# A two-layer Mamba-2 and attention trunk: engines issue in the source's order, with the source laid out anew

## The chip, the cores and the metric

The kernel runs on one core of a Trainium2 chip. The metric is the device time of one execution in microseconds (us). The engines are PE (TensorE, the matrix multiplier, with its weight loads as PEld), DVE (VectorE), ACT (ScalarE), POOL (GpSimd) and SP (SyncE, which here only issues transfers). Every engine works through its own list of instructions in order. A list is fixed when the kernel is built; at run time an instruction waits for semaphores that others raise.

## The reference, cut to what matters

256 tokens of width 2048 pass a Mamba-2 layer and an attention layer, all in float32.

```python
# layer 0: Mamba-2 mixer, then x <- LayerNorm(ALPHA * x + mixer(x))
zxbcdt = x @ w_in                                   # z | x, B, C | dt
xbc = silu(causal_conv4(xbc) + conv_b)
dt = softplus(dt_raw + dt_bias); a = -exp(a_log)
y = ssd_chunked(xs, dt, a, bm, cm) + xs * d_skip    # decays from a cumulative sum of dt * a
y = y * silu(z)
y = y * rsqrt(mean(y**2 within a group) + EPS) * norm_w   # 8 groups
h = y @ w_out
# layer 1: one shared k, v; window of 128 with a sink per head
k, v = x @ kv_w + kv_b;  k = rope(k)
q, gate = x @ w_in;      q = rope(q + q_bias)
h = (softmax_with_sink(q k / 8) v * silu(gate)) @ w_out
# and again x <- LayerNorm(ALPHA * x + h)
```

## The kernel before

**Products.** Every large product is made of three matmuls (`mac`, `out_unit`, `x_stat`): each float32 operand is split into a high part and a low remainder, and high x high, low x high and high x low are added in PSUM. The weights come as *units* of 128 x 2048. `load_unit` (line 122) loads a unit in two halves of 512 KB into `wr` (five buffers, issued by SP, L129), ACT writes the high part `wh` (L137), DVE the remainder `wl` (L138); there are four buffers of each. `next_unit` gives out the next unit, and `fill_units` before it keeps `AHEAD` = 2 units loaded and split beyond those given out.

**Layer 0** runs over eight groups. A group has ten input blocks of 128 columns, each one unit of 48 matmuls of 256 columns (`gemm_ws`): B, C, four x blocks, four z blocks (in group 0 the z blocks first). `conv_silu` evicts a B, C or x block: ACT once (L402), three shifted multiply-adds on DVE (L404), a tanh on ACT (L407), a last DVE operation (L408). `in_z` evicts a z block. A table `plan` names what comes after which block: step t = 10 g + b is block b of group g. In a group: the decays (`sum_decay`, `exp_decay` on ACT, from rows that a transfer has spread over the partitions, `load_decay`, `load_low`); `cb` (two small matmuls on PE, then `cbm` and two large `e` products on DVE, L483 and L486); the turned x times dt (group 0: `tr`, PE transposes L499; others: `turn_blocks`, `load_turned`, `scale_x` by DVE transposes and DRAM); `ymm` (PE, L550, evicted by DVE); `gate` (POOL products L566 to L572, then the split into `yH` on ACT and `yL` on DVE for each block in turn); `norm` (an inverse root by three Newton steps, twelve POOL operations L600 to L603 on 128 x 2). The out products of a group (four units of 24 matmuls of 512 columns, `out_unit`) run among the next group's blocks at `OUT_AT`; their eviction L302 needs the inverse root. PSUM has four `mm` buffers, taken in turn, and four `ax` buffers.

Group 0 begins in `products_first`: three units and the dt columns arrive in nine pieces; PE takes a piece's dt matmuls and then its products. `make_dt` follows: a softplus, a scan over time (L368), two transfers to DRAM (`rscr`), from which `load_decay` reads. `turn_dt` (step 6) transposes dt.

**The boundary.** After group 7 come three more out units of group 6, the norm of group 7, and its four out units in `out_last`: units in turn for row half 0 and, for the first, row half 1; `done1(0)`; the remaining units for half 1; `done1(1)`. `done1(h)` normalises the row half by pieces of 512 (L759, L762), transposes each on PE (L767) and splits it into `x1H` (ACT, L772) and `x1L` (DVE, L773). Then k and v: four units, half 0 and then half 1, 12 matmuls each (`x_stat`, L809 to L811).

**Layer 1** runs over `B_ORDER`: q blocks and gate blocks, out units, and the attention of each pair (`attend`), whose steps are put off by a number of ticks (`later`).

**What sets the order.** Before, each engine's list is laid out by a planner, which orders instructions by priority and its estimate of times; `tc.high_priority` (L401, L472, L644) moves some ahead, and `keep_in_program_order` holds a few. A buffer's next use waits for the release of its last one.

Of the kernel before, what the change touches and what calls it, by code (L numbers as in the profile page):

```python
# [15 lines left out]
P = 128  # L16
S = 256
# [8 lines left out]
AHEAD = 2  # L26

TD, TS, CB0 = 6, 6, 9
# [3 lines left out]
NZERO = 3  # L32
XK_AT = (12, 13)
ZPRI = 200
PRE = 1
CPRI = 0
# [24 lines left out]
def trunk(ctx: ExitStack, tc: tile.TileContext, A: dict, out: bass.AP, dbg=None):  # L61
# [53 lines left out]
    def new_unit(places):  # L115
        u = Unit()
        u.parts = []
        for tag, n, pl in (("wh", NH, places[0]), ("wl", NL, places[1])):
            t = wp.tile([P, 2112], F32R, tag=tag, name=nm(tag), bufs=n)
            u.parts.append([(t[:, o : o + (k1 - k0) * P], k0, k1) for o, k0, k1 in pl])  # L120
        u.h, u.l = u.parts[0][0][0], u.parts[1][0][0]
        return u

    def load_unit(src, places):
        u = new_unit(places)
        raws = []
        for c in range(2):
            raw = wp.tile([P, 1024], F32, tag="wr", name=nm("wr"), bufs=NR)
            nc.sync.dma_start(raw[:], src[:, c * 1024 : (c + 1) * 1024])  # L129
            raws.append(raw)  # L130
        for c in range(2):
            for (h, k0, k1), (l, _, _) in zip(*u.parts):
                a, b = max(k0, 8 * c), min(k1, 8 * c + 8)
                if a < b:
                    sl = slice((a - k0) * P, (b - k0) * P)
                    raw = raws[c][:, (a - 8 * c) * P : (b - 8 * c) * P]
                    nc.scalar.activation(h[:, sl], raw, AF.Copy)  # L137
                    nc.vector.tensor_tensor(l[:, sl], raw, h[:, sl].bitcast(F32), ALU.subtract)  # L138
        return u
# [25 lines left out]
    def products_first():  # L165
# [9 lines left out]
        nc.sync.dma_start(pc[:], A["pc"])  # L175
        fill_units()
        pss = [mm_tile() for _ in us]
        pd = ax_tile()
        for (k0, k1), raw in zip(FIRST, raws):
            for k in range(k0, k1):  # L180
                rows = slice(64 * (k % 2), 64 * (k % 2) + 64)
                nc.tensor.matmul(
                    pd[rows, :S], raw[:, k - k0, FCOL - NHD :], raw[:, k - k0, :S], start=k < 2, stop=k >= KT - 2
                )
# [7 lines left out]
        return pd, pss  # L192
# [13 lines left out]
    srcs += wo_srcs("wo", NG - 1) + [A["wkv"][i] for i in range(4)]  # L206
    broken = set()
    for what, j in B_ORDER:
        if what == "g":
            broken.update(range(len(srcs), len(srcs) + 4))  # L210
        srcs += wo_srcs({"q": "wq", "g": "wg", "o": "wb"}[what], j)
    units = []
    used = [0]

    def fill_units():
        while len(units) < min(used[0] + AHEAD, len(srcs)):
            n = len(units)
            if n == 4:
                nc.sync.dma_start(cc[:], A["cc"])
# [6 lines left out]
            units.append(load_unit(srcs[n], BROKEN if n in broken else [WHOLE, WHOLE]))  # L226

    def next_unit():
        used[0] += 1
        fill_units()  # L230
        return units[used[0] - 1]
# [104 lines left out]
    def make_dt(ps):  # L336
        f = [ap.tile([P, S], F32, tag="sm", name=nm("f"), bufs=NSM) for _ in range(3)]
        f4 = ap.tile([P, 4, S], F32, tag="xs", name=nm("f4"), bufs=1)
        u, e, rec, z = [f4[:, i, :] for i in range(4)]
        w, q, dt = [x[:] for x in f]  # L340
        nc.scalar.copy(e, ps[:, :S])
        both = ax_tile()
        nc.tensor.matmul(both[:, :S], fold, e, start=True, stop=True)
        nc.scalar.activation(u, both[:, :S], AF.Identity, bias=pc[:, PC_DTB : PC_DTB + 1])
        nc.scalar.activation(e, u, AF.Abs)
        nc.scalar.activation(e, e, AF.Exp, scale=-1.0)
        aneg = ap.tile([P, 1], F32, tag="aneg", name="aneg")
        nc.scalar.activation(aneg[:], pc[:, PC_ALOG : PC_ALOG + 1], AF.Exp)
        nc.vector.tensor_scalar(aneg[:], aneg[:], -1.0, None, ALU.mult)
        nc.vector.tensor_scalar(rec, e, 2.0, None, ALU.add)  # L350
        nc.vector.reciprocal(rec, rec)
        nc.vector.tensor_tensor(z, e, rec, ALU.mult)
        nc.vector.tensor_tensor(w, z, z, ALU.mult)
        nc.vector.tensor_scalar(q, w, 1.0 / 15.0, None, ALU.mult)
        nc.vector.tensor_scalar(z, z, 2.0, None, ALU.mult)
        for d in (13.0, 11.0, 9.0, 7.0, 5.0, 3.0):
            nc.vector.scalar_tensor_tensor(q, q, 1.0 / d, w, ALU.add, ALU.mult)
        nc.vector.scalar_tensor_tensor(q, q, 1.0, z, ALU.add, ALU.mult)
        nc.vector.scalar_tensor_tensor(dt, u, 0.0, q, ALU.max, ALU.add)
        da, hi = e, rec  # L360
        nc.vector.tensor_scalar(da, dt, aneg[:], None, ALU.mult)
        nc.vector.tensor_scalar(hi, da, QUANT, None, ALU.add)
        nc.vector.tensor_scalar(hi, hi, QUANT, None, ALU.subtract)
        nc.vector.tensor_tensor(hi[64:128], da[64:128], hi[64:128], ALU.subtract)
        one = z
        nc.gpsimd.memset(one, 1.0)
        rc = w
        nc.vector.tensor_tensor_scan(rc, one, hi, 0.0, ALU.mult, ALU.add)  # L368
        nc.sync.dma_start(rscr[0:64, :], rc[:64])

        nc.scalar.activation(hi[64:128], rc[64:128], AF.Exp)
        nc.sync.dma_start(rscr[64:128, :], hi[64:128])
        return rc, dt, q
# [21 lines left out]
    def conv_silu(ps, t, dst):  # L395
# [5 lines left out]
        with tc.high_priority(CPRI):  # L401
            nc.scalar.activation(a[:], ps[:, :S], AF.Identity, scale=w(3), bias=w(4))  # L402
            for sft in (1, 2, 3):
                nc.vector.scalar_tensor_tensor(  # L404
                    a[:, sft:], ps[:, : S - sft], w(3 - sft), a[:, sft:], ALU.mult, ALU.add
                )
        nc.scalar.activation(dst, a[:], AF.Tanh)  # L407
        nc.vector.scalar_tensor_tensor(dst, dst, 1.0, a[:], ALU.add, ALU.mult)  # L408
# [61 lines left out]
    def in_z(g, i, ps):  # L470
        z = ap.tile([P, S], F32, tag="zz", name=nm("z"), bufs=4)
        with tc.high_priority(ZPRI):  # L472
            nc.scalar.activation(z[:], ps[:, :S], AF.Tanh, scale=0.5)
            nc.vector.scalar_tensor_tensor(z[:], z[:], 1.0, ps[:, :S], ALU.add, ALU.mult)
# [34 lines left out]
    def turn_blocks(g):  # L509

        st = gs[g]
# [51 lines left out]
    def gate(g, i):  # L563
        st = gs[g]
        v = st.yz[:, i, :]
        nc.gpsimd.tensor_tensor(v, v, st.z[i][:], ALU.mult)  # L566
        q = ap.tile([P, S], F32, tag="sm", name=nm("sq"), bufs=NSM)
        nc.gpsimd.tensor_tensor(q[:], v, v, ALU.mult)
        if i == 0:
            st.ss = q  # L570
        else:
            nc.gpsimd.tensor_tensor(st.ss[:], st.ss[:], q[:], ALU.add)  # L572
        if i == 0:
            st.y = (
                yp.tile([P, 4, S], F32R, tag="yH", name=nm("yH"), bufs=2),
                yp.tile([P, 4, S], F32R, tag="yL", name=nm("yL"), bufs=2),
            )
        yH, yL = st.y
        c = PC_NW + g * 4 + i
        nc.scalar.activation(yH[:, i, :], v, AF.Copy, scale=pc[:, c : c + 1])  # L580
        nc.vector.scalar_tensor_tensor(
            yL[:, i, :], v, pc[:, c : c + 1], yH[:, i, :].bitcast(F32), ALU.mult, ALU.subtract
        )

    def norm(g):
# [13 lines left out]
        for _ in range(3):  # L599
            nc.gpsimd.tensor_tensor(t, r, r, ALU.mult)  # L600
            nc.gpsimd.tensor_tensor(t, t, v, ALU.mult)
            nc.gpsimd.tensor_scalar(t, t, -0.5, 1.5, ALU.mult, ALU.add)
            nc.gpsimd.tensor_tensor(r, r, t, ALU.mult)  # L603
        st.rms = r

    def group(g):
# [16 lines left out]
        if g == NG - 1:  # L623
            out_units(g - 1, [1])
            out_units(g - 1, [2, 3])
# [12 lines left out]
    dt_ps, first_ps = products_first()  # L638

    for c0, c1 in ((PC_CONV, PC_CONV + 240), (PC_NW, PC_NW + 32)):  # L640
        nc.vector.tensor_scalar(pc[:, c0:c1], pc[:, c0:c1], 0.5, None, ALU.mult)

    with tc.high_priority():
        dts = make_dt(dt_ps)  # L644
        load_decay(0, 0)

# [3 lines left out]

    def rotary():
        posi = ap.tile([P, 2], I32, tag="posi", name="posi")
        tc.keep_in_program_order(nc.gpsimd.dma_start(posi[:], A["pos"]))
        inv = ap.tile([P, 8], F32, tag="inv", name="inv")
        tc.keep_in_program_order(nc.gpsimd.dma_start(inv[:], A["inv"]))
# [33 lines left out]
    at(35, rotary)  # L689
    for g in range(NG):  # L690
        t = 10 * g
        if g == 0:
            at(TD, turn_dt, *dts)
            at(TS, load_decay, 0, 1)
            at(TS, load_low, 0)
            steps = TS
            pos = dict(cb=CB0, tr=12, y=13, norm=16)
# [24 lines left out]
        for i in range(4):  # L722
            at(t + pos["y"], gate, g, i)
# [22 lines left out]

    with ExitStack() as s2:
# [6 lines left out]
        def done1(h):  # L754
            mv, rs = norm_scale(lp, st1, h)
# [404 lines left out]
```

## Time and profile before

| what | value |
|---|---|
| median of 3 runs | 1000.1 us (999.4 to 1002.09) |
| the profiled execution | 1000.52 us |
| its span, first to last instruction | 998.7 us |
| mean granted TensorE clock | 0.995 |
| PE, DVE, ACT, POOL busy | 984.9, 776.9, 533.7, 202.6 us |

The span is the part of the execution that the profile shows; 1.8 us lie around it. A matmul's busy time includes its way through the array, and the next one starts before it has ended, so PE is counted as busy while it issues at full pace and also where its start-to-start interval is longer than it need be. A row of the table of windows reads: from and to, length, then busy us and count of PE, PEld, DVE, ACT and POOL, the granted clock, the share of the DMA engines and GB/s. A timeline row reads: start, us, engine, line, operation, tiles out<-in, shapes, count of merged instructions, and in brackets the idle time before it with what ended that.

### The profile page before, as it was taken

To read this page: it belongs to the slowest core of one execution; us is meant where nothing else is said; L and a number is where in the kernel's file an instruction comes from. 1 tells how busy PE (TensorE), PEld (TensorE's weight loads), DVE (VectorE), ACT (ScalarE), POOL (GpSimd) and SP (SyncE) were. 2 spreads that over 40 slices of the span, in tenths; PEclk is the share of its full clock that TensorE was granted. 3 is DMA by queue.
4 is the path that set the end of the run, shared out by engine and by line. 5 is a ranking of instruction groups with operands and counts; after the bars stand their busy time and mean duration, and the time that the engine had idled before them with its cause. 6 is when DMAs were issued, how large, how long until landed. Compare 5 with 4: busy or idle time off the path is not lost.

```text
span 998.7 us, 17607 instructions
## 1 busy us (share of the span) xinstructions
PE 984.9 (99%) x6836; PEld 880.7 (88%) x6836; DVE 776.9 (78%) x1147; ACT 533.7 (53%) x901; POOL 202.6 (20%) x321
## 2 busy tenths in 40 slices
PE   9999989999999999999999999999999999999997
PEld 7999979999998999999999999877898878777975
DVE  6769986786897697787788688889657586888786
ACT  6686736545645645644754654444355446444632
POOL 0000323203055120320320311320211303030202
PEclk9999999999999999999999999999999999999998
DMA  9697676686767657648658467555774848484942
GB/s 357 234 298 235 198 242 222 185 258 189 228 193 252 207 181 264 202 158 295 199 163 283 144 222 244 203 190 180 229 246 138 295 149 315 145 302 144 326 159 85
DMA packets 69444, 218.72 MB, mean 219 GB/s; under 512 B 8096, under 2 KB 19632, under 8 KB 68592
## 3 DMA queue, kind: packets, MB, share of 16 engines
q1 hardware_dynamic: 63648, 198.95, 60.9%
q0 software_dynamic: 5424, 18.12, 5.3%
q8 instruction: 54, 0.88, 0.3%
q10 hardware_dynamic: 288, 0.52, 0.1%
q14 instruction: 30, 0.25, 0.1%
HBM read 205.37 MB, written 12.19 MB: 218 GB/s over the span
## 4 chain that ended last, share of the span: by engine, by line
PE 82%; DVE 9%; DMA 4%; ACT 2%; issue 2%; POOL 1%; SPq 0%; DVEq 0%; POOLq 0%; ACTq 0%
PE mm L234 15%; PE mm L235 15%; PE mm L236 15%; PE mm L295 8%; PE mm L296 7%; PE mm L297 7%; PE mm L809 3%; PE mm L811 3%; PE mm L810 3%; DVE wl L138 2%; PE ax L550 2%; PE ax L922 1%; DMA wr<-in_wa 1%; PE ax L980 1%; DVE cv L404 1%
## 5 line engine op out<-in xcount | busy, mean ns | idle before, releaser
L138 DVE TENSOR_TENSOR wl<-wr,wh 128x1024 fp32r<-128x1024 f32 (+2 forms) x338 | 392.9, 1178 | 104.3 <-ACT wh L137 103.5
L137 ACT ACTIVATE wh<-wr 128x1024 fp32r<-128x1024 f32 (+2 forms) x338 | 334.9, 1012 | 201.4 <-PE mm L235 68.1
L234 PE MATMUL mm<-xH,wh 128*128 128x256 f32 x1280 | 355.7, 278 | 0.2 <-ACT wh L161 0.2
L235 PE MATMUL mm<-xL,wh 128*128 128x256 f32 x1280 | 354.5, 277 | 0.0
L236 PE MATMUL mm<-xH,wl 128*128 128x256 f32 x1280 | 354.3, 277 | 0.1
L234 PEld LDWEIGHTS mm<-xH,wh 128*128 128x128 f32 x1280 | 240.4, 188 | 5.0 <-ACT wh L161 2.2
L235 PEld LDWEIGHTS mm<-xL,wh 128*128 128x128 f32 x1280 | 240.4, 188 | 1.2 <-DVE xL L157 0.2
L236 PEld LDWEIGHTS mm<-xH,wl 128*128 128x128 f32 x1280 | 240.3, 188 | 0.4 <-DVE wl L138 0.3
L295 PE MATMUL mm<-wh,yH 128*128 128x512 f32 x256 | 102.0, 399 | 3.5 <-DVE xr L302 3.5
L296 PE MATMUL mm<-wh,yL 128*128 128x512 f32 x256 | 100.6, 393 | 0.0
L297 PE MATMUL mm<-wl,yH 128*128 128x512 f32 x256 | 100.4, 392 | 0.0
L566 POOL TENSOR_TENSOR yz<-yz,z 128x256 f32<-128x256 f32 x32 | 32.7, 1029 | 267.7 <-DVE yz L561 267.7
L404 DVE SCALAR_TENSOR_TENSOR cv<-mm,pc,cv 128x255 f32<-128x255 f32 x144 | 68.5, 476 | 8.9 <-ACT cv L402 7.6
L235 PE MATMUL mm<-x1L,wh 128*128 128x256 f32 x256 | 70.8, 277 | 0.0
L234 PE MATMUL mm<-x1H,wh 128*128 128x256 f32 x256 | 70.8, 276 | 0.0
L236 PE MATMUL mm<-x1H,wl 128*128 128x256 f32 x256 | 70.7, 276 | 0.0
L809 PE MATMUL mm<-wh,x1H 128*128 128x512 f32 x160 | 63.8, 399 | 0.0
L811 PE MATMUL mm<-wl,x1H 128*128 128x512 f32 x160 | 62.7, 392 | 0.5 <-DVE wl L138 0.4
L810 PE MATMUL mm<-wh,x1L 128*128 128x512 f32 x160 | 62.7, 392 | 0.2 <-DVE x1L L773 0.2
L295 PEld LDWEIGHTS mm<-wh,yH 128*128 128x128 f32 x256 | 48.4, 189 | 14.7 <-DVE xr L302 3.4
L302 DVE SCALAR_TENSOR_TENSOR xr<-mm,r,xr 128x512 f32<-128x512 f32 x64 | 46.1, 743 | 16.0 <-POOL r L603 10.0
L297 PEld LDWEIGHTS mm<-wl,yH 128*128 128x128 f32 x256 | 48.5, 189 | 10.3
(214 smaller groups left out, 1378.8 us busy)
## 6 DMA issues: line engine op xcount, KB each, us to landing
wr<-in_wa SPq DMA_DIRECT2D x154, 512.0 KB, 5.2
wr<-in_wo SPq DMA_DIRECT2D x64, 512.0 KB, 4.8
wr<-in_wq SPq DMA_DIRECT2D x32, 512.0 KB, 4.8
wr<-in_wg SPq DMA_DIRECT2D x32, 512.0 KB, 5.0
wr<-in_wb SPq DMA_DIRECT2D x32, 512.0 KB, 5.3
rb<-rscr SPq DMA_DIRECT2D x16, 512.0 KB, 5.3
el<-rscr SPq DMA_DIRECT2D x16, 256.0 KB, 4.9
wr<-in_wkv SPq DMA_DIRECT2D x8, 512.0 KB, 5.9
```

The costliest lines, as they stand in the source:

```text
L137: nc.scalar.activation(h[:, sl], raw, AF.Copy)
L138: nc.vector.tensor_tensor(l[:, sl], raw, h[:, sl].bitcast(F32), ALU.subtract)
L234: nc.tensor.matmul(ps, ah, bh, start=first, stop=False)
L235: nc.tensor.matmul(ps, ah, bl, start=False, stop=False)
L236: nc.tensor.matmul(ps, al, bh, start=False, stop=last)
L295: nc.tensor.matmul(ps[:], aH[:, k, hs], u.h[:, ks], start=k == 0, stop=False)
L296: nc.tensor.matmul(ps[:], aL[:, k, hs], u.h[:, ks], start=False, stop=False)
L297: nc.tensor.matmul(ps[:], aH[:, k, hs], u.l[:, ks], start=False, stop=k == 3)
L404: nc.vector.scalar_tensor_tensor(a[:, sft:], ps[:, : S - sft], w(3 - sft), a[:, sft:], ALU.mult, ALU.add)
L809: nc.tensor.matmul(ps[:], x1H[:, kk, hs], u.h[:, ks], start=kk == 0, stop=False)
L810: nc.tensor.matmul(ps[:], x1L[:, kk, hs], u.h[:, ks], start=False, stop=False)
L811: nc.tensor.matmul(ps[:], x1H[:, kk, hs], u.l[:, ks], start=False, stop=kk == KT - 1)
```

## The change

- All of the kernel stands in a region in which PE, DVE, ACT, POOL and SP issue in the order in which the source names the instructions. The planner's priorities are gone.
- `AHEAD` is 3 from unit 12 on (1 and 2 at the start). Loads are issued half by half: as a half is split, the half five places further on is issued (`load_half`).
- `conv_silu`'s tanh and last operation are put into `posts` and come out at the next `flush`, which `next_unit` calls after `fill_units` (and `turn_blocks` at its head).
- The dt chain is a class `DT`: its matmuls are done at other pieces (`DT_VISITS`), so that they end with piece 6 of 0 to 8; copy after piece 6, fold ahead of piece 7's products, `begin` after the last, `end` at step 3, `turn` at step 5.
- Group 0: `tr` at step 10 and `ymm` at 11 (before: 12 and 13).
- `gate` does all its POOL work in one piece; the split into `yH`, `yL` is `split_y`, two steps later. The Newton steps are nine DVE operations.
- The first two kv units are loaded and split early, among the last out units, into four buffers of their own (`EXTRA`). The boundary's work is listed anew: `root1`, `scale1`, `add1`, `turn_x` and the kv products `kv(h, unit)`.
- In layer 1 the softmax's division is a step of its own (`share_p`, a tick later), and some tiles come from a second pool `bq`.

The diff, cut to its core:

```diff
-AHEAD = 2
-TD, TS, CB0 = 6, 6, 9
+AHEAD = 3
+TD, TS, CB0 = 5, 6, 9
+DT_VISITS = {0: (0, 1), 2: (2,), 3: (3, 4), 5: (5, 6), 6: (7, 8)}
+EXTRA = {("wh", 0), ("wl", 0), ("wh", 1), ("wl", 1)}
...
+    def load_half():
+        if halves:
+            n, c = halves.pop(0)
+            raws[n, c] = raw = wp.tile([P, 1024], F32, tag="wr", name=nm("wr"), bufs=NR)
+            nc.sync.dma_start(raw[:], srcs[n][:, c * 1024 : (c + 1) * 1024])
...
                     nc.scalar.activation(h[:, sl], raw, AF.Copy)
                     nc.vector.tensor_tensor(l[:, sl], raw, h[:, sl].bitcast(F32), ALU.subtract)
+            load_half()
...
     def fill_units():
-        while len(units) < min(used[0] + AHEAD, len(srcs)):
+        while len(units) < min(used[0] + ahead[0], cap[0]):
             n = len(units)
+            if n == 12:
+                ahead[0] = AHEAD
...
     def next_unit():
         used[0] += 1
         fill_units()
+        flush()
         return units[used[0] - 1]
...
+        def rest():
+            nc.scalar.activation(dst, a[:], AF.Tanh)
+            nc.vector.scalar_tensor_tensor(dst, dst, 1.0, a[:], ALU.add, ALU.mult)
+
+        posts.append(rest)
...
         for _ in range(3):
-            nc.gpsimd.tensor_tensor(t, r, r, ALU.mult)
-            nc.gpsimd.tensor_tensor(t, t, v, ALU.mult)
-            nc.gpsimd.tensor_scalar(t, t, -0.5, 1.5, ALU.mult, ALU.add)
-            nc.gpsimd.tensor_tensor(r, r, t, ALU.mult)
+            nc.vector.scalar_tensor_tensor(t, r, -0.5, r, ALU.mult, ALU.mult)
+            nc.vector.tensor_tensor(t, t, v, ALU.mult)
+            nc.vector.scalar_tensor_tensor(r, t, 1.5, r, ALU.add, ALU.mult)
...
         if g == NG - 1:
             out_units(g - 1, [1])
-            out_units(g - 1, [2, 3])
+            out_units(g - 1, [2])
             for t in sorted(plan):
...
-            at(TD, turn_dt, *dts)
-            at(TS, load_decay, 0, 1)
-            at(TS, load_low, 0)
+            at(3, dts.end)
+            at(TD, dts.turn)
+            at(TD, load_decay, 0, 1)
+            at(TD, load_low, 0)
             steps = TS
-            pos = dict(cb=CB0, tr=12, y=13, norm=16)
+            pos = dict(cb=CB0, tr=10, y=11, norm=16)
...
-        for i in range(4):
-            at(t + pos["y"], gate, g, i)
+        at(t + pos["y"], gate, g)
+        at(t + pos["y"] + 2, split_y, g)
...
+    prefetch(len_a)
+    cap[0] = len_a
+    out_units(NG - 2, [3])
+    prefetch(len_a + 1)
...
+        for nb in range(4):
+            us.append(next_unit())
+            add1(0, nb)
+        root1(0)
+        more(2)
+        scale1(0, 0)
+        add1(1, 0)
+        scale1(0, 1)
+        add1(1, 1)
+        turn_x(0, 0)
+        more(3)
+        scale1(0, 2)
+        add1(1, 2)
+        turn_x(0, 1)
+        scale1(0, 3)
+        add1(1, 3)
+        turn_x(0, 2)
+        more(4)
+        root1(1)
...
+    kv(0, 0)
+    turn_x(0, 3)
+    scale1(1, 0)
+    kv(0, 1)
+    scale1(1, 1)
+    kv(0, 2)
+    ahead[0] = 1
+    fill_units()
+    scale1(1, 2)
+    kv(0, 3)
+    turn_x(1, 0)
+    scale1(1, 3)
+    kv(1, 0)
+    turn_x(1, 1)
+    ahead[0] = 2
+    fill_units()
+    kv(1, 1)
+    turn_x(1, 2)
+    kv(1, 2)
+    turn_x(1, 3)
+    kv(1, 3)
...
-        trunk(tc, args, out)
+        E = _mybir.EngineType
+        with tc.manual_schedule(engines={E.PE, E.DVE, E.Activation, E.Pool, E.SP}):
+            trunk(tc, args, out)
```

`add1(h, nb)` is an `out_unit` of group 7 with its statistics, `root1` the inverse deviation, `scale1` the two DVE operations of one piece, `turn_x` the transposes with the split, and `more(n)` splits kv units up to the n-th.

More of the change, by code (lines that the diff above doesn't have):

```diff
@@ L334, in trunk @@
     rscr = dram.tile([P, S], F32, tag="rscr", name="rscr")
[L336 to L373, printed above, removed]
@@ L509, in turn_blocks @@
     def turn_blocks(g):
+        flush()
         st = gs[g]
@@ L997, in pv @@
             nc.vector.tensor_tensor(oL[:, :, hs], o[:], oH[:, :, hs].bitcast(F32), ALU.subtract)
+        later(1, share_p)
         later(2, turn_p)
```

325 lines of the change are left out of this document (212 added, 113 removed).

## The prediction

> **What bounds the kernel now.** The page's busy row comes first.
>
> ```profile
> PE 984.9 (99%) x6836; PEld 880.7 (88%) x6836; DVE 776.9 (78%) x1147; ACT 533.7 (53%) x901; POOL 202.6 (20%) x321
> ```
>
> TensorE (PE) is in use nearly always, so only its holes can be won, and any new hole is lost in full. In the table of windows I looked for stretches where PE (the first number after the length) falls short of the 25 us.
>
> ```profile
> 50.00:75.00 25.00, 24.09 (x204) 23.47 (x203) 16.66 (x29) 20.47 (x37) 0.00 (x0) 1.00 0.91 298
> 75.00:100.00 25.00, 24.54 (x219) 23.07 (x218) 24.74 (x36) 15.38 (x22) 0.00 (x0) 1.00 0.73 235
> 125.00:150.00 25.00, 22.04 (x132) 19.34 (x131) 20.88 (x23) 9.98 (x11) 4.91 (x12) 0.93 0.71 243
> 650.00:675.00 25.00, 23.64 (x111) 18.77 (x110) 22.00 (x33) 10.81 (x14) 5.78 (x15) 1.00 0.51 179
> 675.00:700.00 25.00, 23.93 (x108) 18.40 (x107) 24.12 (x44) 11.18 (x14) 2.28 (x3) 1.00 0.57 187
> ```
>
> Apart from the first and last 25 us, these five rows hold almost all the lost time: 0.91 + 0.46 + 2.96 us in the first group and 1.36 + 1.07 us where the two layers meet. The other 33 windows are full or miss at most 0.11 us. VectorE (DVE, third number) is near saturation in 75 to 100 and in 675 to 700. The hole at 125 has a second part, which the chain of waits shows.
>
> ```profile
> 131.66 0.50 PE mm L295
> ...
> 133.10 0.43 PE mm L296
> 133.53 0.43 PE mm L297
> ```
>
> These 512-column matmuls follow at 0.43 us; elsewhere they follow at 0.23 (next part). Eight of them after the 2.96 us hole cost 8 x 0.20 = 1.6 us, and this is the window whose granted clock is 0.93.
>
> **The change part by part.** *Group 0's first chain.* The dt softplus and scan now start from products finished two pieces earlier, go out in one run on DVE (`end`, step 3), and are transposed at step 5. The 50 and 75 holes were waits for that chain and for the lagging DVE behind it; I cost their removal at 0.91 + 0.46 = 1.4 us. At least 0, if a new wait takes their place (the next item).
>
> *The inverse root on DVE.* The out products of group 0 stood 2.96 us because their eviction (L302) waited for POOL's twelve Newton steps. These become nine DVE operations. The row of a similar small one:
>
> ```profile
> L598 DVE TENSOR_SCALAR r<-r 128x2 int32<-128x2 int32 x8 | 1.3, 167 | 0.2
> ```
>
> So 9 x 0.17 = 1.5 us on DVE per group, 12 us in all, spread over groups in which DVE has about a fifth of its time free; PE pays nothing there. This removes 2.96 + 1.6 = 4.6 us. With the first item the gain is 5.9 us, up to 6.5 if drain tails counted as busy go too.
>
> *Transposes of group 0 moved from step 12 to 10.* Here the source's order bites. The last x block is evicted at step 9; its closing tanh and DVE operation (`rest`) are held in `posts` until the next `next_unit`, which calls `fill_units` before `flush`. At step 10 exactly, unit 12 raises the look-ahead from 2 to 3, so two units are split, not one. DVE therefore issues in order: three shifted adds, `cbm` and two `e` products (step 9), four half splits, and only then `rest`. PE issues `cb`, one block, then `tr`, which needs `rest`. The prices, from the timelines of DVE and PE:
>
> ```profile
> 75.88 0.55 DVE L483 TENSOR_TENSOR cbm<-ax,cc 128x384 f32<-128x384 f32 x1
> 76.35 0.47 DVE L404 SCALAR_TENSOR_TENSOR cv<-mm,pc,cv 128x254 f32<-128x254 f32 x1
> 76.74 1.75 DVE L486 TENSOR_TENSOR e<-e,cbm 128x1536 f32<-128x1536 f32 x1
> 78.40 0.47 DVE L404 SCALAR_TENSOR_TENSOR cv<-mm,pc,cv 128x253 f32<-128x253 f32 x1
> 78.79 1.75 DVE L486 TENSOR_TENSOR e<-e,cbm 128x1536 f32<-128x1536 f32 x1
> 80.46 0.42 DVE L408 SCALAR_TENSOR_TENSOR xs<-xs,cv 128x256 f32<-128x256 f32 x1
> 80.80 2.35 DVE L138 TENSOR_TENSOR wl<-wr,wh 128x1024 fp32r<-128x1024 f32 x2
> 83.07 0.47 DVE L404 SCALAR_TENSOR_TENSOR cv<-mm,pc,cv 128x255 f32<-128x255 f32 x1
> ```
>
> ```profile
> 69.99 0.59 PE L481 MATMUL ax<-ct,bt 128*128 128x256 f32 x2
> 70.42 0.38 PE L482 MATMUL ax<-ct,bt 128*128 128x128 f32 x2
> 70.56 0.36 PE L234 MATMUL mm<-xH,wh 128*128 128x256 f32 x1
> ...
> 87.19 0.28 PE L235 MATMUL mm<-xL,wh 128*128 128x256 f32 x1
> 87.30 0.28 PE L236 MATMUL mm<-xH,wl 128*128 128x256 f32 x1
> 87.42 1.04 PE L499 MATMUL ax<-cc,xs 128*128 128x128 f32 x8
> ```
>
> From start to start: `cbm` 0.47, an add 0.39, an `e` product 1.66, a pair of half splits 2.27, `rest` 0.34. Counted from the end of PE's block of step 9, DVE ends `rest` after about 0.6 (eviction on ACT, signals; an estimate below the 0.60 of a copy twice as wide, shown later) + 3 x 0.39 + 0.47 + 2 x 1.66 + 2 x 2.27 + 0.34 = 10.4 us. PE arrives after 0.57 (`cb`) + 48 matmuls at 0.113 (two intervals above are 0.11 and 0.12) = 5.4 + six of eight transposes, at most 1.04 x 6/8 = 0.8, together 6.8. PE then stands 3.7 us. ACT, which sums and exponentiates the decays in steps 6 to 8, can only make it later. The hole is longer than the one at 125, so I add its 1.6 us of slow matmuls: 5.3 us. Bounds: nothing, if DVE gets through earlier than I think; 7 us, with ACT late by 1.5.
>
> The Trainium skill ("TensorE: Matmul & The Clock Gate", Part 1) has the clock halve after one idle window of about 3.4 us. The row here shows it after 2.96 us. By the page alone a 3.7 us hole need not cover a whole free-running window, and the price would be 3.7 instead of 5.3 us.
>
> *Look-ahead of 3, loads half by half, gate in one piece in the other groups.* A unit is split three units before its use, so DVE and ACT may lag two blocks (10.9 us) before PE notices. The heaviest DVE step, 4, holds norm 1.5, `cb` 3.8, two splits, two evictions; by the prices above it runs at most 4 us late. Cost 0 from cover; an uncovered lag would cost what exceeds 10.9 us. SP is passed by the `rscr`, `zd` and `xt` transfers in source order and waits for each, with five half loads and three split units in hand: 0.
>
> *Where the layers meet.* Two kv units are split ahead into four more buffers. The order becomes row half 0, then row half 1 mixed with normalising and kv. The stretch from the first of three last out units to the first K transpose is one row of the windows (from PE's L295 at 627.90 to L836 at 707.60).
>
> ```profile
> 627.90:707.60 79.70, 77.28 (x351) 61.75 (x350) 69.24 (x104) 33.49 (x43) 19.52 (x31) 1.00 0.58 203
> ```
>
> It holds 24 x 3 + 96 + 96 + 48 = 312 matmuls at 0.227, eight transpose groups of 0.36 and a small sum: 74.1 us; the rest, 5.6 us, are stalls. In the new order `turn_x(1, c)` stands on PE directly ahead of `kv(1, c)`, which needs it. What that costs, from one such turn in the timeline (PE, ACT, DVE):
>
> ```profile
> 685.56 0.60 PE L767 MATMUL ax<-cc,xr 128*128 128x128 f32 x4
> ...
> 686.20 0.60 ACT L772 ACTIVATE x1H<-ax 128x512 fp32r<-128x512 f32 x1 [2.27 <-PE ax L767]
> ...
> 687.03 0.68 DVE L773 TENSOR_TENSOR x1L<-ax,x1H 128x512 fp32r<-128x512 f32 x1
> ```
>
> PE can go on at 685.92, x1L is there at 687.71, with a free DVE 0.2 earlier; one matmul (0.23) needs x1H alone. So 1.4 us a turn. Before, the turn is followed by matmuls that don't need it; now four turns expose it: 5.6 us, all that could be won. Beside it DVE must reach x1L(1, 0) in time:
>
> ```profile
> 658.04 1.39 DVE L302 SCALAR_TENSOR_TENSOR xr<-mm,r,xr 128x512 f32<-128x512 f32 x2
> 659.35 1.28 DVE L737 BATCH_NORM_STATS2 st<-xr 128x6 f32<-128x512 f32 x2
> ...
> 681.12 1.40 DVE L762 SCALAR_TENSOR_TENSOR xr<-t,rs,gb 128x512 f32<-128x512 f32 x2
> ```
>
> In order it has nine splits (20.4), 14 evictions (0.66 each, 9.2), eight statistics (4.8), seven scalings (1.35 each, 9.4), five x1L (3.1), the tail of `ymm`, `split_y` and norm (about 6.5): 53.4 us from the start of the stretch, and a few waits. PE is there after 16.7 (out units) + 21.8 (adds) + 10.9 (kv, half 0) + 1.8 (turns) = 51.2. I take 1.3 us for this and 1.3 us for turns (0, 2) and (0, 3), which follow their scaling closely: 8.2 against 5.6, so 2.6 us lost. Bounds: 0 and 5.
>
> *Attention and the end.* `share_p` a step later takes DVE's wait for ACT's exponentials off the queue; PE shows no hole there. The tail's source order is the one already run. 0 both.
>
> **Sum.** The profiled execution took 1000.5 us (span 998.7 and 1.8 around it). 1000.5 - 5.9 + 5.3 + 2.6 = 1002.5; the median of the runs shown is 0.4 lower, so 1002.1 us: gains spent on two new holes.
>
> **The rivals.** *A, the holes stay small.* If DVE reaches `rest` with PE (it would have to be 3.7 us quicker than the source's order allows) and the boundary breaks even, 1000.1 - 5.9 = 994.2. For it: DVE is idle a third of 50 to 75, and the dt chain starts earlier; against it: in-order DVE can't use idle time for work queued behind a wait. *B, DVE slows down beside GpSimd.* `gate` now sends its eleven POOL operations as one block.
>
> ```profile
> 106.11 1.63 DVE L138 TENSOR_TENSOR wl<-wr,wh 128x1024 fp32r<-128x1024 f32 x1
> 106.62 1.72 POOL L566 TENSOR_TENSOR yz<-yz,z 128x256 f32<-128x256 f32 x1
> ```
>
> A half split of 1.13 takes 1.63 there. Over the some 9 us of the last group's gate, DVE would lose up to 9 x (1 - 1.13/1.63) = 2.8 us just ahead of the boundary, where it has a margin of under 1 us (the split of the last out unit ends as PE asks for it). From that point each us is PE's: 1002.1 + 2.8 = 1004.9, slower. The Trainium skill ("SBUF — State Buffer", Who interferes with whom) says that a DVE operation with two SBUF inputs and a GpSimd operation that reads SBUF exclude each other for a whole instruction; these two rows agree. *C, the order does nothing*, because the planner's order was nearly the source's: then only the norm gain stays, 1000.1 - 4.6 = 995.5; against it stand the many transposes and splits that the profile shows out of source order.
>
> **How the numbers follow.** Forecast (997 to 1004 by itself) 0.45, A 0.25, B 0.25, C 0.05. Likeliest time 1002.1. The range reaches from A's 994 to B with a boundary at its bound of 5: 994 to 1009. A measurement can tell about 0.3% (3 us: 997.1 to 1003.1) from no change. Faster: A and C, and little of the forecast: 0.31. Same: most of the forecast and a bit of B: 0.36. Slower: most of B and the forecast's upper end: 0.33.
>
> **What would show it.** PE idle near 75 us ahead of L499's counterpart, released by the DVE `rest`, followed by matmuls at half pace; no hole at 125; no Newton steps on POOL; four gaps of 1.4 us between row half 1's transposes and their kv products, and about 82 us for the stretch that took 79.70. It is wrong if the first is missing, if the groups in the middle show holes, or if attention does.

## The result and the profile after

The changed kernel takes 1037.2 us (median of 4 runs, 1032.6 to 1038.2) beside 1000.3 us for the kernel before (999.4 to 1002.1): ratio 1.0358, 95% interval 1.0323 to 1.0392. The prediction was 1002.1 us with a range up to 1009, so it was wrong. The profiled execution is the shortest of the four, 1032.6 us with a span of 1030.9.

First the page's busy row of the changed kernel, then its table of windows, in the order of columns of before.

```profile
PE 992.2 (96%) x6836; PEld 887.5 (86%) x6836; DVE 799.7 (78%) x1219; ACT 531.9 (52%) x901; POOL 168.6 (16%) x225
```

```profile
50.00:75.00 25.00, 25.00 (x220) 24.95 (x219) 19.30 (x27) 20.52 (x36) 0.00 (x0) 1.00 0.84 270
75.00:100.00 25.00, 19.99 (x161) 18.88 (x160) 21.09 (x32) 12.33 (x15) 7.41 (x8) 0.86 0.76 273
125.00:150.00 25.00, 25.00 (x170) 22.80 (x170) 24.09 (x34) 11.11 (x12) 0.00 (x0) 1.00 0.93 312
650.00:675.00 25.00, 21.50 (x97) 16.63 (x97) 21.68 (x30) 8.45 (x12) 0.54 (x1) 1.00 0.53 181
675.00:700.00 25.00, 20.55 (x80) 15.43 (x79) 18.26 (x25) 7.96 (x12) 0.00 (x0) 0.86 0.33 111
825.00:850.00 25.00, 22.29 (x155) 20.30 (x154) 16.21 (x37) 17.31 (x52) 3.51 (x7) 0.94 0.34 109
875.00:900.00 25.00, 19.60 (x104) 15.45 (x100) 15.29 (x25) 14.22 (x46) 0.00 (x0) 0.96 0.30 90
900.00:925.00 25.00, 22.20 (x87) 18.20 (x88) 23.05 (x39) 8.14 (x8) 11.72 (x20) 0.83 0.87 290
...
628.33:720.74 92.41, 81.51 (x351) 63.61 (x350) 73.07 (x113) 32.40 (x42) 15.07 (x18) 0.96 0.49 166
```

The holes of before at 50 and 125 are gone, as forecast. Three losses are new: one at 75, the boundary (the last row; the same stretch of work took 79.70 us before), and attention, where before every window but the last was full or missed at most 0.11 us. Two of its rows before the change:

```profile
825.00:850.00 25.00, 25.00 (x173) 22.22 (x173) 15.73 (x26) 14.43 (x25) 9.52 (x16) 1.00 0.85 304
875.00:900.00 25.00, 25.00 (x109) 19.27 (x108) 20.77 (x35) 13.51 (x29) 9.53 (x16) 1.00 0.91 307
```

DVE's busy time grew by 23 us, but where PE stands most, DVE is idle too (busy 15.29 of 25 us at 875): the engines wait for one another.

The span cut at two places that both kernels have, the first of the last three out units (627.90 before, 628.33 after) and the first K transpose (707.60 and 720.74), gives the account that the rest of this text uses:

| us | layer 0 | boundary | attention and end | span |
|---|---|---|---|---|
| before | 627.9 | 79.7 | 291.1 | 998.7 |
| after | 628.3 | 92.4 | 310.1 | 1030.9 |
| difference | +0.4 | +12.7 | +19.0 | +32.1 |
| predicted | -0.6 | +2.6 | 0 | +2.0 |

The timeline of PE (changed kernel) shows the three largest holes and what follows them.

```profile
74.68 0.82 PE L574 MATMUL ax<-cc,xs 128*128 128x128 f32 x6
80.51 0.69 PE L574 MATMUL ax<-cc,xs 128*128 128x128 f32 x2 [5.01 <-DVE xs L482]
80.85 0.56 PE L288 MATMUL mm<-xH,wh 128*128 128x256 f32 x1
81.21 0.41 PE L289 MATMUL mm<-xL,wh 128*128 128x256 f32 x1
81.42 0.41 PE L290 MATMUL mm<-xH,wl 128*128 128x256 f32 x1
...
687.27 0.49 PE L929 MATMUL mm<-wh,x1H 128*128 128x512 f32 x1 [0.69 <-ACT x1H L843]
690.58 0.79 PE L930 MATMUL mm<-wh,x1L 128*128 128x512 f32 x1 [2.82 <-DVE x1L L844]
691.17 0.63 PE L931 MATMUL mm<-wl,x1H 128*128 128x512 f32 x1
691.60 0.63 PE L929 MATMUL mm<-wh,x1H 128*128 128x512 f32 x1
...
697.18 0.49 PE L929 MATMUL mm<-wh,x1H 128*128 128x512 f32 x1 [0.69 <-ACT x1H L843]
697.90 0.50 PE L930 MATMUL mm<-wh,x1L 128*128 128x512 f32 x1 [0.23 <-DVE x1L L844]
...
902.80 0.77 PE L349 MATMUL mm<-wh,oH 128*128 128x512 f32 x1 [8.20 <-DVE qt L1004]
903.36 0.63 PE L350 MATMUL mm<-wh,oL 128*128 128x512 f32 x1
```

Behind each hole the starts lie twice as far apart (0.21 us instead of 0.11 for 256 columns, 0.43 instead of 0.23 for 512). The last hole is the telling one: an out product waits for a PSUM tile that the eviction of q (L1004, DVE) has yet to empty. The timeline of ACT and DVE ahead of it:

```profile
881.01 0.17 DVE L1087 TENSOR_TENSOR sm<-snk,sm 128x8 f32<-128x8 f32 x1
881.21 0.21 ACT L1088 ACTIVATE sm<-sm 128x8 f32<-128x8 f32 x1 [3.82 <-DVE sm L1087]
...
884.47 2.00 ACT L148 ACTIVATE wh<-wr 128x1024 fp32r<-128x1024 f32 x2
885.55 2.36 DVE L149 TENSOR_TENSOR wl<-wr,wh 128x1024 fp32r<-128x1024 f32 x2 [4.37 <-ACT wh L148]
...
892.72 0.21 ACT L1088 ACTIVATE sm<-sm 128x8 f32<-128x8 f32 x1 [5.20 <-DVE sm L1087]
...
895.91 4.83 ACT L148 ACTIVATE wh<-wr 128x1024 fp32r<-128x1024 f32 x5
896.99 2.36 DVE L149 TENSOR_TENSOR wl<-wr,wh 128x1024 fp32r<-128x1024 f32 x2 [4.30 <-ACT wh L148]
...
901.97 0.68 DVE L1004 TENSOR_TENSOR qt<-mm,bias 128x512 f32<-128x512 f32 x1
```

ACT stands at its list's head until DVE has the row maximum (3.82 us), then does nine exponentials, and only then splits the weights that stood behind them. DVE in turn stands for that split (4.37 us), with the rest of the softmax and the evictions of q behind it. Twice in a row, and L1004 comes 8 us after PE asked.

### The profile page after: what moved, and what is told of

Same layout as the page of the kernel before. It is cut to its first block, busy times and chain, and to the rows that moved or that the text cites. A ratio compares the mean times of both kernels' runs of the same rounds, so it can differ in the third digit from the quotient of the medians.

```text
span 1030.9 us, 17547 instructions
## 1 busy us (share of the span) xinstructions
PE 992.2 (96%) x6836; PEld 887.5 (86%) x6836; DVE 799.7 (78%) x1219; ACT 531.9 (52%) x901; POOL 168.6 (16%) x225
## 4 chain that ended last, share of the span: by engine, by line
PE 74%; DVE 11%; DMA 6%; ACT 5%; issue 3%; POOL 0%; SPq 0%; DVEq 0%; POOLq 0%; ACTq 0%
PE mm L288 14%; PE mm L289 14%; PE mm L290 14%; PE mm L349 7%; PE mm L350 7%; PE mm L351 7%; DVE wl L149 4%; PE ax L626 2%; PE mm L930 2%; ACT wh L148 2%; DMA wr<-in_wq 2%; PE mm L931 2%; PE mm L929 2%; ACT p L1090 2%; DMA wr<-in_wa 1%
## 5 line engine op out<-in xcount | busy, mean ns | idle before, releaser
L148 ACT ACTIVATE wh<-wr 128x1024 fp32r<-128x1024 f32 (+2 forms) x338 | 327.9, 1011 | 199.4 <-PE mm L350 74.0
L476 DVE SCALAR_TENSOR_TENSOR cv<-mm,pc,cv 128x255 f32<-128x255 f32 x144 | 69.1, 480 | 19.4 <-ACT cv L474 15.9
L474 ACT ACTIVATE cv<-mm,pc 128x256 f32<-128x256 f32 x48 | 26.9, 560 | 72.0 <-PE mm L290 72.0
L349 PE MATMUL mm<-wh,oH 128*128 128x512 f32 x128 | 51.6, 403 | 8.2 <-DVE qt L1004 8.2
```

Of the source, the lines that this page charges most:

```text
L349: nc.tensor.matmul(ps[:], aH[:, k, hs], u.h[:, ks], start=k == 0, stop=False)
L476: nc.vector.scalar_tensor_tensor(a[:, sft:], ps[:, : S - sft], w(3 - sft), a[:, sft:], ALU.mult, ALU.add)
```

## The experiments

Theory 1: ACT's and DVE's lists in the source's order make attention slow. Rivals: loads that land late, or PE's own order. For the boundary: exposed turns against a DVE slowed beside GpSimd. For the hole at 75: the splits ahead of the closing operation against DVE's whole list. Each ratio is to the kernel before on the same chip and goes by all executions; the parts of the span are those of the table above, from the one execution that was profiled, and the changed kernel's are 628.3, 92.4 and 310.1. Words behind a # in the cuts of code below are remarks, and `...` marks what is left out.

| run | ratio (95%) | layer 0 | boundary | rest |
|---|---|---|---|---|
| planner, new source | 1.0106 (1.0084 to 1.0128) | 633.5 | 82.1 | 296.5 |
| planner from attention on | 1.0104 (1.0080 to 1.0128) | 627.7 | 82.7 | 300.2 |
| same, ACT and DVE alone | 1.0059 (1.0039 to 1.0080) | 627.2 | 84.1 | 298.6 |
| q evicted ahead of the tick | 1.0310 (1.0283 to 1.0336) | 627.7 | 92.5 | 314.9 |
| exponentials behind the split | 1.0058 (1.0037 to 1.0079) | 628.0 | 92.8 | 290.0 |
| turns earlier | 1.0200 (1.0153 to 1.0246) | 627.5 | 84.1 | 310.5 |
| closing operations first | 1.0289 (1.0243 to 1.0335) | 627.7 | 94.6 | 311.1 |
| all three | 1.0001 (0.9976 to 1.0025) | 631.9 | 83.2 | 289.9 |
| transposes at step 11 | 1.0253 (1.0213 to 1.0294) | 625.0 | 90.1 | 313.5 |
| step 11, turns, exponentials | 0.9957 (0.9941 to 0.9973) | 625.2 | 83.3 | 290.2 |
| and third kv split later | 0.9966 (0.9949 to 0.9982) | 623.9 | 84.6 | 289.6 |
| and out products later | 0.9929 (0.9912 to 0.9946) | 620.3 | 84.4 | 289.9 |
| and squares on ACT | 0.9933 (0.9913 to 0.9954) | 622.5 | 82.5 | 290.1 |
| and both | 0.9906 (0.9885 to 0.9927) | 620.4 | 81.8 | 290.2 |

**Is it the order?** Three runs hand all or part of the program back to the planner (the load of an activation table is kept in its place in them).

```diff
+    region.close()                # planner from attention on
     kv_stack.close()
...
+    region.close()                # ACT and DVE alone
+    region.enter_context(tc.manual_schedule(engines={PE, Pool, SP}))
     kv_stack.close()
...
-        with tc.manual_schedule(engines={E.PE, E.DVE, E.Activation, E.Pool, E.SP}):
-            trunk(tc, args, out)  # planner, new source
+        trunk(tc, args, out)
```

Planner from attention on:

> Source order ends with the kv products; attention, gates and the closing norm are again ordered by the planner. Theory 1 (the lists of ACT and DVE, in source order, hold q's evictions and the split halves behind the softmax): from the first K transpose to the end about 292 us instead of 310, in all about 1019, no PE hole over 2 us after the K transposes. Rival 2 (loads come late, or the pool of attention tiles that opens only after the kv products): the 310 stay, 1035 or more.

ACT and DVE alone planned there:

> As the run before, but only ACT's and DVE's lists are planned in attention; PE, POOL and SP keep the source's order there. Theory 1 (ACT's and DVE's lists): about 1019, within 3 us of the run before. Rival 3 (it is PE's own order, with scores, PV products and turns at fixed places, or the DMA issues of POOL): 1030 or more.

All planned, new source:

> The new source with its four more buffers, its reordered chains, its norm on DVE and its look-ahead, but all engines ordered by the planner as before. If the order alone is what costs: 994 to 1001, boundary stretch 75 to 82 us, no hole of 5 us at the transposes of group 0. If the new source itself costs (prefetched kv loads, the later pool, look-ahead of 3): 1005 or more, with the boundary near 90.

Attention fell by 10 us with the planner and by 11.6 with ACT and DVE alone planned. So the order of these two lists is the cause. PE's order is not: from the first K transpose to the end, PE's timelines name the same tiles in the same order before the change, after it and in both of these runs. Neither run came down to the 291 of before: in the first, holes of 4.15 us (a product of probabilities and v that waited for a transfer) and 2.21 us (the second K transposes) were left. The boundary fell too, by 8 to 10 us, which nobody expected of an edit behind it: with the region closed, the planner put products of the next q unit between the kv products, where PE had stood. The second of these runs therefore did not keep PE's order at the boundary as it was meant to. The new source under the planner met neither expectation in full: its boundary (82.1) is near the old one, but layer 0 is 5.6 us longer than before, attention 5.4, and the ratio 1.0106. By these runs the order is most of the loss, not all. Whether the rest is the new source itself, or the planner without the priorities that the old source gave it, no run shows.

**Which part of the attention lists?** Two runs move one thing each: the first q's evictions, the second the exponentials, which `next_unit` then issues behind its split (`fill_units`, then `flush`).

```diff
             for h in range(2):
                 x_stat(pss[h], h, u, ui)
-            tick()
+            if ui < 3:
+                tick()
+        qts = []
         for h in range(2):
...
             nc.vector.tensor_tensor(qf, pss[h][:], qb[:], ALU.add)
+            qts.append((qt, qf))
+        tick()
+        for h in range(2):
+            qt, qf = qts[h]
             rope(qt[:], h, 8)
```

> Everything in source order; only the two evictions of a q block stand ahead of its last tick instead of behind it, and so ahead of that tick's softmax and the next split. Theory 1: the PE holes at 843.7 (2.9 us) and 894.2 (8.4 us, with some 2 us of slow matmuls behind it) go or fall below 1 us: 1024 to 1028. Rival (the hole is the splits', held behind eight exponentials, and merely shows at the eviction): the hole moves to the next matmul that needs a wh or wl, and at most 3 us are won, 1034 or more.

```diff
-        nc.scalar.activation(es, es, AF.Exp)
-        for r in range(8):
...
+        def exps():
+            nc.scalar.activation(es, es, AF.Exp)
+            for r in range(8):
...
+        posts.append(exps)

         def share_p():
+            flush()
```

> Source order everywhere; only the nine exponentials of a softmax part are issued behind the next unit's split instead of ahead of it. Theory 1 (ACT stands in its list for the row maximum, the split behind it comes late, DVE stands for that split, and q's evictions behind it come late on PE): ACT's 41 us of waiting for the row maximum between 740 and 990 falls below 15, DVE's 54 us of waiting for wh falls by 20 or more, the 8.4 us hole at 894 goes, from the last of the first 192 x_stat matmuls to the end about 262 us instead of 272: 1025 to 1029. Rival (loads come late in attention, ACT waits 46 us for them): the wait for DMA takes the place of the wait for the row maximum, 1033 or more.

The eviction alone won nothing (1.0310, and 314.9 us for the rest of the span). Its rival had the time right, but not the place: the 8.2 us of idle became 5.4, still ahead of the out product that waits for the eviction of q, and the products of probabilities and v then stood 3.5 and 4.3 us. With the exponentials behind the split the rest is 290.0, below the 291.1 of before. The mechanism was as expected and the gain, 20 us, twice the 10 that were expected. The views of the waits between 740 and 990 (engine, line, waited for; us, times, longest), changed kernel and then this run:

```profile
ACT sm L1088 <- DVE sm L1087: 40.9, 8, 7.8
ACT wh L148 <- DMA wr<-in_wq: 30.9, 12, 6.7
...
DVE wl L149 <- ACT wh L148: 54.2, 32, 4.4
```

```profile
ACT sm L1089 <- DVE sm L1087: 15.0, 8, 2.4
ACT wh L148 <- DMA wr<-in_wq: 13.7, 9, 2.8
...
DVE wl L149 <- ACT wh L148: 21.8, 22, 3.2
```

ACT's wait for the row maximum and DVE's for the split fell by 26 and 32 us; before the change the second was 18.9 (`DVE wl L138 <- ACT wh L137`). The wait for loads fell as well: each load is issued when an older half has been split, so late loads were a consequence. That rules out the rival, by which this wait would have grown. The timeline of DVE in this run has the eviction of q 17.7 us earlier, 4 us behind the last of its matmuls instead of 13:

```profile
879.24 2.35 DVE L149 TENSOR_TENSOR wl<-wr,wh 128x1024 fp32r<-128x1024 f32 x2
...
884.26 0.68 DVE L1004 TENSOR_TENSOR qt<-mm,bias 128x512 f32<-128x512 f32 x1
```

No wait now stands ahead of DVE's split there. By the profiles the run is 20.1 us shorter than the changed kernel, by the two ratios to the kernel before about 30: the changed kernel's profile was its shortest run, and this one's (1012.6 us) near its longest (1007.7 to 1012.8).

**The boundary.** Each turn of row half 1 goes one kv product earlier, so that 12 matmuls lie between a turn and its product.

```diff
     kv(0, 2)
+    turn_x(1, 0)
...
     kv(0, 3)
-    turn_x(1, 0)
+    turn_x(1, 1)
...
     kv(1, 0)
-    turn_x(1, 1)
+    turn_x(1, 2)
...
     kv(1, 1)
-    turn_x(1, 2)
+    turn_x(1, 3)
     kv(1, 2)
-    turn_x(1, 3)
```

> Source order everywhere; each turn of row half 1 stands one kv product earlier, so PE has 12 matmuls (2.7 us) between a turn and the product that needs it. Theory (the boundary's loss is the exposed way PE to ACT to DVE to PE, with the hole of 2.8 us and the slow matmuls behind it): the stretch of 92.3 us falls to 82 to 84 and the kernel to 1027 to 1030. Rival (DVE, slowed beside GpSimd or with the splits ahead of its scalings, is late anyway): the holes stay ahead of the same kv products, stretch 89 or more, 1034 or more.

The row of the windows for the stretch in this run, to be held against 92.41:

```profile
627.49:711.59 84.10, 76.89 (x350) 61.67 (x349) 72.98 (x113) 32.52 (x42) 15.08 (x18) 1.00 0.53 180
```

8.3 us were won, the granted clock is 1.00 again, and DVE's busy time is the same 73 us: most of the loss was not DVE's amount of work, but that PE had nothing to do while it answered. DVE is still late in places: among the kv products one hole of 1.52 us is left, ahead of a turn that waits for its scaling, and the holes of 0.7 and 1.9 us ahead of turns of row half 0 stay.

**The hole at 75.** One run issues the closing operations ahead of the split, another leaves PE one block more.

```diff
         used[0] += 1
+        flush()
         fill_units()
-        flush()
...
-            pos = dict(cb=CB0, tr=10, y=11, norm=16)
+            pos = dict(cb=CB0, tr=11, y=12, norm=16)
```

Closing operations first:

> Source order everywhere; a step's held closing operations are issued ahead of the next split instead of behind it. The prediction's reading (transposes of group 0 wait for the closing operation that stands behind two units' splits): the hole of 5.0 us at 75 falls below 1 us, the slow matmuls behind it go, and the start of group 1's decay products comes 5 to 7 us earlier: 1030 to 1032. Rival (DVE is behind by its other work, e products above all): the hole shrinks by under 2 us, and other holes open because ACT's splits come later: 1035 to 1039.

Transposes at step 11:

> Source order everywhere; only group 0's transposes stand at step 11 and its decay products and gate at step 12, one block (5.4 us of PE work) later than in the changed kernel. Theory (the hole of 5.0 us at 75 is DVE reaching the last x block late, by its whole list of that step, not by the splits alone): one block more on PE covers it, the hole falls below 1 us, the start of group 1's decay products moves from 153 to 146 to 148: 1029 to 1032. Rival (the lag is only passed on: decay products or the out products of group 0 at 131 then wait): the start stays above 150, 1034 or more.

The hole only shrank from 5.01 to 4.08 us in the first, though the four half splits (4.62 us) no longer stand ahead of the closing operation. DVE's timeline in that run:

```profile
63.40 0.42 DVE L482 SCALAR_TENSOR_TENSOR xs<-xs,cv 128x256 f32<-128x256 f32 x1 [2.07 <-ACT xs L481]
...
71.91 1.51 DVE L476 SCALAR_TENSOR_TENSOR cv<-mm,pc,cv 128x255 f32<-128x255 f32 x3
...
73.92 3.43 DVE L561 TENSOR_TENSOR e<-e,cbm 128x1536 f32<-128x1536 f32 x2
77.27 0.42 DVE L482 SCALAR_TENSOR_TENSOR xs<-xs,cv 128x256 f32<-128x256 f32 x1
```

In the changed kernel the last three adds (L476) began at 70.14 and the `e` products (L561) at 72.15. Now DVE waits in the steps before for ACT's tanh and for the split behind it (2.07 us in the first row), and is 1.8 us later at the same place: what the order gives here it takes in those steps. This run's total lies below the changed kernel's, but its profile is not shorter, so where that came from stays open. The block more does cover the hole (the window 75 to 100 has PE busy 24.89 us), but group 0's gate is a step later too, and its out products then stand 2.16 us at 126, with 1.5 us of slow matmuls behind. Of 7.1 us (5.01 and 21 matmuls that each lost 0.10), 3.3 were won, so the lag is in part passed on, as its rival said.

**Put together.** All three edits at once, the closing operations first in layer 0 only; then the transposes at step 11 in their place; then two tries to better that.

All three:

> The three edits together (closing operations ahead of the split only in layer 0, so that the exponentials stay behind it). If the three losses are separate terms, as the prediction's sum has it: 1037 - 10 - 9 - 6 = 1012, give or take 4. If one lag passes from stage to stage (work put off in one stage is late in the next): 1020 or more.

Step 11, turns, exponentials:

> The earlier turns and the exponentials behind the split, as in the run with all three, but with the transposes of group 0 at step 11 in place of the closing operations ahead of the split. If the layer 0 loss of that run (products of the last group 4 us later than before the change) goes: 994 to 999 on a chip where the kernel before takes 1001, ratio 0.993 to 0.998, attention 286 us as before the change, boundary 83. If the source's order costs DVE time everywhere: 1001 or more.

The same, with the third kv unit split later:

```diff
         turn_x(0, 0)
-        more(3)
...
         turn_x(0, 2)
+        more(3)
         more(4)
```

> As the run before, and the third kv unit is split after the last turn of row half 0 instead of between its first and second. Theory (in the boundary DVE is behind by a split pair of 2.35 us when the turns of half 0 come): the holes of 0.8 and 2.1 us ahead of these turns go, stretch 80 to 81: 2 to 3 us below the run before. Rival (DVE has no idle time there, so the split is only paid later, ahead of the kv product that needs it): stretch 83, no difference above 1 us.

The boundary and attention kept their gains in all of them (83.2 and 289.9): these two terms add. Layer 0 did not: its list is that of the run with the closing operations first, yet it takes 631.9 us instead of 627.7. The hole at 131 was 2.72 us with 15 slow matmuls (2.6 us) behind it here, and 1.66 with none there. Such a hole near the point where the clock drops makes a scatter of some 4 us by itself. With the transposes at step 11 the kernel is faster than before the change, 0.9957. The later split won nothing: the hole of 0.7 us ahead of the first turn stayed, and those of 1.9 us ahead of the third and 1.5 us ahead of the fifth were gathered into one of 3.78 ahead of the fifth. DVE has next to no idle time there to put the split in.

**The rest of the boundary, and the hole at 126.**

```diff
-OUT_AT = [[], [6, 7, 8, 9]] + ...
+OUT_AT = [[], [7, 8, 9]] + ...
...
-            nc.gpsimd.tensor_tensor(q[:], v, v, ALU.mult)
+            nc.scalar.activation(q[:], v, AF.Square)   # last group, from posts
```

Out products later:

> The version with earlier turns, exponentials behind the split and transposes at step 11, with group 0's out products one block later (their first at block 7 of group 1, the fourth behind its last block). Theory (the 2.6 us hole at 126 with some 1.6 us of slow matmuls is the norm, which now comes a block after a later gate): hole below 0.5 us, 3 to 4 us less, ratio 0.991 to 0.993. Rival (the eviction waits for DVE's whole list, not for the norm): the hole moves with the products, no difference above 1 us.

Squares on ACT:

> The version with earlier turns, exponentials behind the split and transposes at step 11, with the last group's four squares on ACT behind the next split in place of POOL (four POOL operations fewer beside DVE's splits at 628 to 637). Rival B of the prediction (DVE, slowed beside GpSimd's gate, is late into the boundary): DVE's split pairs there return from 3.3 towards 2.35 us, the holes at 636, 661 and 669 (1.1 + 0.7 + 1.9 us) shrink by 2 us or more, stretch 81. If DVE is late by the amount of its own work: the stretch changes by less than 1 us.

Both:

> Both edits of the two runs before. Separate terms: the sum of their gains, within 1 us.

One block later the out products find their norm: no hole at 126, layer 0 5.0 us shorter. The squares bear on rival B of the prediction. DVE's timeline in the changed kernel, then with the squares on ACT:

```profile
630.65 3.43 DVE L149 TENSOR_TENSOR wl<-wr,wh 128x1024 fp32r<-128x1024 f32 x2
...
635.33 3.26 DVE L149 TENSOR_TENSOR wl<-wr,wh 128x1024 fp32r<-128x1024 f32 x2
```

```profile
624.86 3.43 DVE L149 TENSOR_TENSOR wl<-wr,wh 128x1024 fp32r<-128x1024 f32 x2
...
630.33 2.43 DVE L149 TENSOR_TENSOR wl<-wr,wh 128x1024 fp32r<-128x1024 f32 x2 [0.72 <-ACT wh L148]
```

Without the squares beside it the second pair takes 2.43; the first, beside the POOL products of y and z that stay, takes 3.43 in both. So DVE is slowed beside GpSimd, by 0.9 to 1.1 us a pair (a pair alone takes 2.35), as B said: 2.0 us for the two, where B had up to 2.8. The Trainium skill ("SBUF — State Buffer", Who interferes with whom) lets a DVE operation with two SBUF inputs and a GpSimd operation that reads SBUF block each other; these rows agree. But the stretch only fell from 83.3 to 82.5: the hole that goes is the norm's wait for the gate's sum (1.1 us), and those ahead of the turns (0.7, 1.9 and 1.5) stay. B's mechanism is there; as far as the squares go, it does not decide the boundary. What the other half, beside the products of y and z, is worth was not tried. The other 2.7 us by which this run is shorter lie in layer 0, ahead of the edit: the hole at 126 is 1.77 us with no slow matmuls here, and 2.62 us with 1.6 us of them in the run without the edit. That is the scatter again. Both edits together take 994.6 us where the kernel before takes 1004.0: 0.9906, the best of all. The ratio falls by 0.0051, and by 0.0028 and 0.0024 for each edit alone, so the gains add as expected, though each holds some of the scatter.

## Why the prediction was wrong, step by step

**Right.** The first chain (1.4 us) and the inverse root on DVE (4.6 us): windows 50 and 125 are full, the clock at 125 is 1.00. Look-ahead and half loads in the middle groups, 0: group 1's decay products to the last three out units took 475.3 us before (152.6 to 627.9) and 475.3 after (153.0 to 628.3). The hole at 75 stood where it was forecast and with that releaser, as 5.0 + 2.1 us instead of 3.7 + 1.6, at the bound of 7. Its mechanism was half right: the splits do stand ahead, but taking them away won 0.9 us, because ACT and DVE are coupled in every step before. That layer 0 as a whole came out near its forecast (+0.4 for -0.6 us) is in part luck: the hole cost 1.8 us more than its term, and some 0.8 us more were won elsewhere in the first group than the sum gives.

**Mis-sized: the boundary, 2.6 predicted, 12.7 measured.** Work is 74.1 us, so 18.3 are stalls instead of 8.2. Turns: an exposed one cost 1.4 us, as predicted (from one kv product to the next 4.64 to 4.68 us, and 3.22 in the run with the turns earlier). The first kv product of half 1 waited 2.8 for `x1L` instead of 0.2, so DVE was 2.6 late, not 1.3; the prediction's own sum of DVE's work (53.4 us against PE's 51.2) gave 2.2, and it took 1.3 without saying why. That hole also brought half-pace matmuls, 11 x 0.20 = 2.2, for which the sum had nothing, though it had priced them after the hole at 75. Most of the rest is in the first half, nearly 7 us up to 678 where 1.3 was given: the norm waits 1.1 for POOL, the split of the last out unit 0.9, the turns of half 0 2.6 for their scalings. The bound of 5 stands in the prediction without a sum.

**The step that failed: "Attention and the end ... 0 both".** It was argued that PE shows no hole there. That was a fact of the planner's order, not of the source's. The prediction had named holes in attention as a sign of being wrong, but gave the step 0 and no bound. Measured: +19.0 us; over PE's timeline the intervals beyond the usual one sum to 15.5 us of holes and 3.7 us in 26 half-pace matmuls. The edit named in that step, `share_p` a tick later, did no harm that can be seen (with it in place attention takes 290.0). What cost the 19 us is the order of the nine exponentials and the split. It is unchanged in the source, but before, the planner and not the source set what was issued; with the two swapped the 310.1 us become 290.0. The method that found the hole at 75, reading DVE's list in source order across a stage, was not applied to layer 1. None of the rivals had this mechanism: A (holes stay small) and C (the order does nothing) are refuted by the windows, B is above, and all three left attention at its time. The range could not have held it: its upper end, 1009, is B with the boundary at 5 and the hole at 75 at 7, and nothing for attention.

## What to carry to other kernels

When an order made by a planner is replaced by the source's, cost every stage anew, also those whose source hardly changed: full windows prove the old order only. In each engine's list look for an operation that waits for another engine and has work behind it that waits for nothing; put that work first (here one such swap was worth 20 us). On TensorE keep independent matmuls between a transpose and the product that needs its copy, and price a hole with the slow matmuls behind it.

## What the runs showed of the hardware

TensorE's half pace follows shorter holes than expected. PE's timeline in the run with the out products later, and then a row of its windows (the granted clock is the third from the end):

```profile
648.62 0.50 PE L349 MATMUL mm<-wh,yH 128*128 128x512 f32 x1 [1.72 <-ACT wh L148]
648.95 0.40 PE L350 MATMUL mm<-wh,yL 128*128 128x512 f32 x1
649.87 0.69 PE L351 MATMUL mm<-wl,yH 128*128 128x512 f32 x1 [0.53 <-DVE wl L149]
650.36 0.63 PE L349 MATMUL mm<-wh,yH 128*128 128x512 f32 x1
```

```profile
650.00:652.00 2.00, 2.00 (x5) 1.60 (x6) 1.97 (x3) 0.00 (x0) 0.00 (x0) 0.51 0.67 219
```

Idle times of 1.72 and 0.53 us, with two matmuls between them, were enough for 3.4 us at half clock (649.87 to 653.3). The Trainium skill ("TensorE: Matmul & The Clock Gate", Part 1) has the clock fall after a whole idle window of about 3.4 us; here and at 687 (2.82 us) PE was never idle that long, so by these runs it takes less than a whole window. Two others had no slow matmuls behind them: 1.91 us at 672 in the changed kernel, and 1.41 and 0.52 us, again with two matmuls between, at 655 in the run with the turns earlier. What decides is not settled.
